# A 31-tap causal convolution rebuilt as three half-length filters on even and odd tokens, with a second u buffer and one weight remainder moved to VectorE

## The chip, the cores and the metric

The program runs on one core of one Trainium2 chip. The metric is the device time of one execution, in microseconds (us), median of several runs.

## The reference, cut to what matters

Three transformer-like blocks follow each other on a 1024 x 1024 activation (1024 tokens, width 1024, float32). The change lies in the input half of the second one: a wide projection, a gated product `a`, and a causal depthwise convolution of 31 taps over the tokens.

```python
    u = _rmsnorm(h, norm_g[l]) * (1.0 + scale) + shift
    proj = u @ w_in[l]
    ...
    a = conv_a * jax.nn.sigmoid(conv_bp)
    a = _causal_depthwise_conv(a, conv_w[l], conv_b[l])     # y[t] = b + sum_j w[j] * a[t - 30 + j], by channel
    a = jax.nn.silu(_layernorm(a, conv_ln_g[l], conv_ln_b[l]))
    a = a @ conv_pw[l]
    y_conv = a * jax.nn.silu(conv_gate)
    q = _rotary(q)
    k = _rotary(k) * (RET_QK_DIM ** -0.5)
    r = _retention_chunkwise(q, k, v)
```

## The kernel before

Activations lie with the channels on the 128 partitions and the tokens along the free dimension: eight tiles of 128 x 1024. A float32 product is made of three float32r matmuls of 128 x 512: weight high part by x high and by x low (L638, L639 in a mixed group), weight low part by x high (L640). ScalarE rounds a weight to its high part `whi` (L159); another engine subtracts to get the low part `wlo` (L160).

The wide projection of block 2 runs as 24 "mixed groups" (class `Mixed`). A group is two output tiles of 128 channels, computed by seven half-size products in place of eight, named a11, a12, s2, s1, s3, s4, a22 in the order in which they run. Each is 12 matmuls of 128 x 512. Products a11, s2, s3 and a22 accumulate in one bank `pb`; it is read out between them: ScalarE copies a11 into half of tile `g` (L653) and s2 into the other (L657), VectorE adds s3 to half of tile `u` (L650), and a22 goes to the other half of `u` (L1180). a12 and the pair s1, s4 use two banks `pa`: ScalarE copies s1 into `u` (L659), VectorE adds a12 and s4 to `g` (L650). So s4 can't begin before the copy of s1 into `u` is done.

The weights of a group come in two loads of 512 KB on SyncE's queue into `raw` (three buffers). GpSimd makes the sums that the products need, in place in `raw`: L607, L609 (s2), L612 (s4, over a12) and L615 (s3). From the third group on, GpSimd also makes all seven low parts (`on_pool = Mixed.ORDER`). `whi` and `wlo` hold two products each and have two buffers.

The groups come in this order: two gates, two "conv" groups, then six times a conv group and two of q, k, v, and two gates. After a conv group, VectorE multiplies the halves into `A[c]` (tile `cv`, L1201), a tile with 30 columns of zeros ahead of the tokens. After a q or k group, `turned` rotates g and u: eight products on VectorE (L1210 to L1214), four sums on GpSimd (L1213, L1215), and two stores on SyncE's queue, from g and u. Tile `g` has two buffers and `u` one.

The taps of the convolution fill VectorE's time between. Each tile c puts 31 jobs into the list `core.bg`, of which `worked` takes as many as `core.rate` says for each product: 2 for a product (RT = 8), 1.5 in q and k groups (RQ = 6). A job is one instruction of 128 x 1024 that multiplies a shifted `A[c]` by a column of weights and adds to an accumulator `acc` of two PSUM banks (L1149 for the first, L1153 for the others). A scheduler settles the order on each engine when the program is built; a job is only kept behind the latest matmul if on TensorE, and behind the latest paced gather if on VectorE.

Behind this stage come the retention loop, in which the convolved tiles are normalized over the channels (`ln_sum` to `ln_scale`), and a product with `conv_pw`.

Of the kernel before, what the change touches and what calls it, by code (L numbers as in the profile page):

```python
# [16 lines left out]
P = 128  # L17
S = 1024
# [11 lines left out]


SB = 6
RQ = 6
RT = 8
NS = 2
VA = 0
VB = 4
# [20 lines left out]
class Core:  # L58
# [40 lines left out]
        self.psm = self.lent.enter_context(self.tc.tile_pool(name=name, bufs=1, space=PSUM))  # L99

    def psum(self, tag, shape=(P, HALF)):
        pool, bufs = {"mm": (self.psm, 3), "acc": (self.psm, 1), "pa": (self.ps, 2), "pb": (self.ps, 2), "pc": (self.ps, 1)}[tag]
        return pool.tile(list(shape), F32, tag=tag, name=self.nm(tag), bufs=bufs)


# [1027 lines left out]
def block2(core, X, scratch, tabs, keep, after):  # L1133
# [7 lines left out]
    with ExitStack() as st:  # L1141
        cvp = st.enter_context(tc.tile_pool(name="b2_conv", bufs=1, reuse_waits="tile"))
        A = [cvp.tile([P, PAD + S], F32, tag=f"a{c}", name=f"cv_{c}") for c in range(KT)]

        def tap(c, j, state):
            def run():
                if j == 0:
                    state["acc"] = core.psum("acc", (P, S))
                    nc.vector.tensor_scalar(state["acc"], A[c][:, :S], core.vec("conv_w_2", c),  # L1149
                                            core.vec("conv_b_2", c), ALU.mult, ALU.add)  # L1150
                    return
                out = A[c][:, PAD:] if j == CW - 1 else state["acc"]
                nc.vector.scalar_tensor_tensor(out, A[c][:, j:j + S], core.vec("conv_w_2", j * KT + c), state["acc"],  # L1153
                                               ALU.mult, ALU.add)
            return run

        at = {}
        core.rate = RT
# [1 line left out]
        with tc.tile_pool(name="b2_mix", bufs=1, reuse_waits="tile") as pool:  # L1160
            cos = pool.tile([P, S], F32, tag="cos", name="cos")
            sin = pool.tile([P, S], F32, tag="sin", name="sin")
            nc.sync.dma_start(cos, ins["tab_cos"])
            nc.sync.dma_start(sin, ins["tab_sin"])
            temp = lambda: pool.tile([P, HALF], F32, tag="t", name=core.nm("rt"), bufs=2)
            turns = []

            def product(f, name):
                at[f, name] = mix.product(plan[f][2], name, x)

            def gather(f, name):
                kind, i, _ = plan[f]
                if name == "a11":
                    at[f, "g"] = tp.tile([P, S], F32, tag="g", name=core.nm("g"), bufs=2)
                if name == "s1":
                    at[f, "u"] = tp.tile([P, S], F32, tag="u", name=core.nm("u"), bufs=1)
                g, u = at[f, "g"], at.get((f, "u"))
                of = {"gate": AF.Silu, "conv": AF.Sigmoid}.get(kind, AF.Copy)
                mix.gather(name, at[f, name], (halves(g), halves(u) if u is not None else (None, None)),
                           lambda u1, ps: nc.scalar.activation(u1, ps, of))  # L1180
                if name in ("a12", "s3", "s4"):
                    core.paced = mix.last
                if kind == "gate":
                    if name == "s4":
                        gate(i, 0, g, slice(0, S))
                    elif name == "a22":
                        gate(i, 1, u, hs(1))
                elif name == "a22":
                    {"conv": conv, "q": turned, "k": turned, "v": values}[kind](kind, i, g, u)
                if name in ("a12", "s2"):  # L1190
                    while turns and len(turns) > (2 if name == "a12" else 0):
                        turns.pop(0)()

            def gate(i, k, y, rest):
                nc.scalar.activation(y[:, rest], y[:, rest], AF.Silu)
                nc.sync.dma_start(heads["gate"][i, :, k], y)

            def conv(_, c, a, b):
                nc.vector.memset(A[c][:, :PAD], 0.0)
                nc.scalar.activation(b[:, hs(1)], b[:, hs(1)], AF.Sigmoid)  # L1200
                nc.vector.tensor_tensor(A[c][:, PAD:], a, b, ALU.mult)  # L1201
                state = {}
                core.bg += [tap(c, j, state) for j in range(CW)]
                core.bg += [lambda: ready.append(c)]

            def turned(kind, i, a, b):
                for half in range(2):
                    sl = hs(half)
                    t1, t2 = temp(), temp()
                    nc.vector.tensor_tensor(t1, a[:, sl], sin[:, sl], ALU.mult)  # L1210
                    nc.vector.tensor_tensor(a[:, sl], a[:, sl], cos[:, sl], ALU.mult)
                    nc.vector.tensor_tensor(t2, b[:, sl], sin[:, sl], ALU.mult)
                    nc.gpsimd.tensor_tensor(a[:, sl], a[:, sl], t2, ALU.subtract)  # L1213
                    nc.vector.tensor_tensor(b[:, sl], b[:, sl], cos[:, sl], ALU.mult)  # L1214
                    nc.gpsimd.tensor_tensor(b[:, sl], b[:, sl], t1, ALU.add)  # L1215
# [12 lines left out]

            ready = []
            mix.early(product, gather)  # L1230
            mix.on_pool = Mixed.ORDER
            for f in range(2, len(plan) - 1):
                core.rate = RQ if plan[f][0] in "qk" else RT
                for name in Mixed.ORDER:
                    product(f, name)
                    gather(f, name)

            f += 1
            core.rate = RT
# [12 lines left out]
            for name in ("s4", "a22"):  # L1252
                gather(f, name)
            while turns:
                turns.pop(0)()
            core.paced = None
            core.drain()
        scratch["mixed"].close()
        core.banks()
        with tc.tile_pool(name="b2_ret", bufs=1, reuse_waits="tile") as pool:  # L1260
            ln = {}

            def ln_sum(c):
                if c == 0:
                    return
                if c == 1:
                    ln["acc"] = pool.tile([P, S], F32, tag="lnacc", name="ln_acc")
                nc.gpsimd.tensor_tensor(ln["acc"], A[0][:, PAD:] if c == 1 else ln["acc"], A[c][:, PAD:], ALU.add)

            def ln_mean():  # L1270
                ln["mu"] = pool.tile([P, S], F32, tag="lnmu", name="ln_mu")
# [3 lines left out]
                    nc.scalar.activation(ln["mu"][:, hs(half)], mu, AF.Copy)  # L1275

            def ln_center(c):
                a = A[c][:, PAD:]
                nc.vector.tensor_tensor(a, a, ln["mu"], ALU.subtract)
                if c == 0:  # L1280
                    ln["var"] = pool.tile([P, S], F32, tag="lnacc", name="ln_var")
                    nc.scalar.activation(ln["var"], a, AF.Square)
                else:
                    sq = core.raw()
                    nc.scalar.activation(sq, a, AF.Square)
                    nc.gpsimd.tensor_tensor(ln["var"], ln["var"], sq, ALU.add)

            def ln_rstd():
# [6 lines left out]
                ln["rb"] = core.over_partitions(ln["r"], pool, tag="lnmu")  # L1295

            def ln_scale(c):
                a = A[c][:, PAD:]
                nc.vector.tensor_tensor(a, a, ln["rb"], ALU.mult)
                nc.scalar.activation(a, a, AF.Silu, bias=core.vec("conv_ln_b_2", c), scale=core.vec("conv_ln_g_2", c))  # L1300

            om = pool.tile([P, P], F32, tag="onesm", name="onesm")
# [137 lines left out]
            core.rate = 0  # L1440
        for half in range(2):
            for c in range(KT):
                core.split(X[c][:, 0, hs(half)], X[c][:, 1, hs(half)], A[c][:, PAD + half * HALF:PAD + (half + 1) * HALF])
        st.close()
        gp = keep.enter_context(tc.tile_pool(name="b2_g", bufs=1, side="right", reuse_waits="tile"))
        G = [gp.tile([P, 2, S], R32, tag=f"g{c}", name=f"yc_{c}") for c in range(KT)]
# [1217 lines left out]
```

## Time and profile before

| | |
|---|---|
| runs of the kernel | 3717.8, 3723.08, 3727.68 us; median 3723.08 |
| profiled execution | 3721.68 us, span of the trace 3719.8 us, mean granted clock 0.961 |
| busy, share of the span | TensorE 93%, its weight loads 75%, VectorE 70%, GpSimd 46%, ScalarE 42% |
| the stage of the 22 looped groups | from 1612 to 2110 us of the span |

The span runs from the first to the last instruction of the trace; 1.9 us of the execution lie around it. TensorE is busy through nearly all of it, so what a stage costs beyond its matmuls is read from TensorE's waits and from its granted clock in that stage.

### The profile page before, as it was taken

To read this page: it belongs to the slowest core of one execution; us is meant where nothing else is said; L and a number is where in the kernel's file an instruction comes from. 1 tells how busy PE (TensorE), PEld (TensorE's weight loads), DVE (VectorE), ACT (ScalarE), POOL (GpSimd) and SP (SyncE) were. 2 spreads that over 40 slices of the span, in tenths; PEclk is the share of its full clock that TensorE was granted. 3 is DMA by queue.
4 is the path that set the end of the run, shared out by engine and by line. 5 is a ranking of instruction groups with operands and counts; after the bars stand their busy time and mean duration, and the time that the engine had idled before them with its cause. 6 is when DMAs were issued, how large, how long until landed. Compare 5 with 4: busy or idle time off the path is not lost.

```text
span 3719.8 us, 45673 instructions
## 1 busy us (share of the span) xinstructions
PE 3448.3 (93%) x16540; PEld 2777.5 (75%) x16540; DVE 2604.3 (70%) x3332; ACT 1567.2 (42%) x2737; POOL 1714.2 (46%) x1398
## 2 busy tenths in 40 slices
PE   8999989899998999899889989889898999899998
PEld 7878777777776778677667778668676788677776
DVE  7888897777776655759988765774559765655644
ACT  5666674433334444532223344224443235553335
POOL 2343343456554533567777653434556442431122
PEclk9999999999999999899999999999899999899999
DMA  4101016333325423322222354466352344325513
GB/s 144 38 30 38 28 63 223 119 107 103 96 94 184 125 74 119 108 80 74 77 76 69 122 156 130 116 194 201 128 161 86 92 122 128 102 80 181 181 48 111
DMA packets 431132, 409.84 MB, mean 110 GB/s; under 512 B 34059, under 2 KB 364347, under 8 KB 430907
## 3 DMA queue, kind: packets, MB, share of 16 engines
q1 hardware_dynamic: 396164, 330.27, 28.8%
q0 software_dynamic: 21088, 68.19, 5.1%
q10 hardware_dynamic: 13655, 8.46, 0.8%
q8 instruction: 131, 2.15, 0.2%
q14 instruction: 94, 0.77, 0.1%
HBM read 284.80 MB, written 122.03 MB: 109 GB/s over the span
## 4 chain that ended last, share of the span: by engine, by line
PE 63%; DVE 15%; DMA 8%; POOL 6%; issue 5%; ACT 3%; SPq 0%; ACTq 0%; POOLq 0%; DVEq 0%
PE mm L236 10%; PE mm L234 10%; PE mm L235 10%; PE pb L638 4%; PE pb L640 4%; PE pb L639 4%; DVE wlo L160 3%; PE pa L638 3%; PE pa L640 3%; PE pa L639 3%; POOL wlo L160 2%; DMA raw<-in_w_in_dram 1%; DMA zy<-zraw_dram 1%; ACT whi L159 1%; DVE x L160 1%
## 5 line engine op out<-in xcount | busy, mean ns | idle before, releaser
L159 ACT ACTIVATE whi<-raw 128x512 fp32r<-128x512 f32 (+3 forms) x610 | 431.8, 737 | 802.1 <-PE pb L639 188.5
L160 DVE TENSOR_TENSOR wlo<-raw,whi 128x512 fp32r<-128x512 f32 (+3 forms) x402 | 503.8, 1273 | 187.9 <-ACT whi L159 184.9
L234 PE MATMUL mm<-x,whi 128*128 128x512 f32 x1152 | 462.7, 402 | 9.0 <-ACT whi L159 3.6
L236 PE MATMUL mm<-x,wlo 128*128 128x512 f32 x1152 | 458.4, 399 | 6.0 <-DVE wlo L160 6.0
L235 PE MATMUL mm<-x,whi 128*128 128x512 f32 x1152 | 460.9, 400 | 0.5 <-DVE x L163 0.2
L160 POOL TENSOR_TENSOR wlo<-raw,whi 128x512 fp32r<-128x512 f32 x208 | 288.0, 1403 | 116.5 <-ACT whi L159 116.4
L493 POOL TENSOR_TENSOR s<-s,f 128x127 f32<-128x127 f32 (+1 forms) x192 | 194.3, 1019 | 293.7 <-DVE f L492 187.4
L1153 DVE SCALAR_TENSOR_TENSOR acc<-cv,par,acc 128x1024 f32<-128x1024 f32 x232 | 298.0, 1285 | 4.3
L638 PE MATMUL pa<-x,whi 128*128 128x512 f32 x648 | 261.1, 403 | 19.5 <-ACT u L659 12.3
L234 PE MATMUL mm<-yc,whi 128*128 128x512 f32 (+1 forms) x656 | 267.8, 409 | 7.3 <-ACT whi L159 6.0
L235 PE MATMUL mm<-yc,whi 128*128 128x512 f32 (+1 forms) x656 | 265.5, 405 | 5.6 <-DVE yc L160 5.5
L640 PE MATMUL pa<-x,wlo 128*128 128x512 f32 x648 | 260.0, 401 | 9.9 <-DVE wlo L160 9.8
L236 PE MATMUL mm<-yc,wlo 128*128 128x512 f32 (+1 forms) x656 | 264.6, 405 | 3.6 <-DVE wlo L160 3.5
L639 PE MATMUL pa<-x,whi 128*128 128x512 f32 x648 | 259.2, 400 | 6.6 <-DVE x L160 6.6
L640 PE MATMUL pb<-x,wlo 128*128 128x512 f32 x576 | 234.2, 412 | 29.8 <-POOL wlo L160 21.6
L234 PEld LDWEIGHTS mm<-x,whi 128*128 128x128 f32 x1152 | 220.0, 191 | 55.6 <-ACT whi L159 4.1
L638 PE MATMUL pb<-x,whi 128*128 128x512 f32 x576 | 237.2, 412 | 25.8 <-ACT whi L159 8.8
L236 PEld LDWEIGHTS mm<-x,wlo 128*128 128x128 f32 x1152 | 219.2, 190 | 52.9 <-DVE wlo L160 7.5
L235 PEld LDWEIGHTS mm<-x,whi 128*128 128x128 f32 x1152 | 219.8, 191 | 45.5 <-DVE x L163 0.6
L639 PE MATMUL pb<-x,whi 128*128 128x512 f32 x576 | 235.1, 408 | 3.5 <-DVE x L160 3.5
L492 DVE TENSOR_TENSOR_SCAN f<-f 128x128 f32<-128x128 f32 (+1 forms) x192 | 195.7, 1033 | 39.0 <-ACT f L485 37.9
L607 POOL TENSOR_TENSOR raw<-raw 128x512 f32<-128x512 f32 x66 | 92.5, 1402 | 275.3 <-DMA raw<-in_ffn_w_in_dram 131.6
(617 smaller groups left out, 8355.2 us busy)
## 6 DMA issues: line engine op xcount, KB each, us to landing
raw<-in_w_in_dram SPq DMA_DIRECT2D x96, 512.0 KB
raw<-in_ffn_w_in_dram SPq DMA_DIRECT2D x44, 512.0 KB
raw<-in_w_out_dram SPq DMA_DIRECT2D x32, 512.0 KB
g<-g_dram SPq DMA_DIRECT2D x56, 256.0 KB
raw<-in_sb_w_in_dram SPq DMA_DIRECT2D x24, 512.0 KB
raw<-in_ada_w_dram SPq DMA_DIRECT2D x24, 512.0 KB
raw<-h_dram SPq DMA_DIRECT2D x18, 512.0 KB
g_dram<-t POOLq DMA_DIRECT2D x8, 1024.0 KB, 4.7
```

Source lines behind the costliest of these rows:

```text
L159: nc.scalar.activation(hi, src, AF.Copy)
L160: return (eng or nc.vector).tensor_tensor(lo, src, hi.bitcast(F32), ALU.subtract).ins
L234: nc.tensor.matmul(ps, w_h, x[:, 0, sl], start=start and k == 0, stop=False)
L235: nc.tensor.matmul(ps, w_h, x[:, 1, sl], start=False, stop=False)
L236: self.last = nc.tensor.matmul(ps, w_l, x[:, 0, sl], start=False, stop=stop and k == n - 1).ins
L492: nc.vector.tensor_tensor_scan(rev, rev, rev, 1.0, ALU.mult, ALU.bypass)
L493: nc.gpsimd.tensor_tensor(s[:, :m - 1], s[:, :m - 1], f[:, 1:m], ALU.mult)
L607: self.eng.tensor_tensor(at["s1"], at["a21"], at["a22"], ALU.add)
L638: nc.tensor.matmul(ps, hi[:, i], x[i][:, 0], start=first and i == 0, stop=False, skip_group_check=more)
L639: nc.tensor.matmul(ps, hi[:, i], x[i][:, 1], start=False, stop=False, skip_group_check=more)
L640: self.core.last = nc.tensor.matmul(ps, lo[:, i], x[i][:, 0], start=False, stop=i == self.N - 1, skip_group_check=more).ins
L1153: nc.vector.scalar_tensor_tensor(out, A[c][:, j:j + S], core.vec("conv_w_2", j * KT + c), state["acc"], ALU.mult, ALU.add)
```

## The change

The 31 taps on 1024 tokens become three filters on 512. `A[c]` holds the even tokens and the odd tokens apart, each with 15 zeros ahead. With x0, x1 the two sequences and o = -(w1, w3, ...) on x1 plus the bias, the program computes the even outputs from the even taps (16) on x0 minus o (15 taps), and the odd outputs from the sums of neighbouring taps (16) on x0 + x1, corrected by the same two filters. It takes 15 + 16 + 16 taps of 128 x 512, and of these the first of the odd and the first of the even filter go to ScalarE (`odd_first`, `even_first`); `sums`, `both` and `even` are four further VectorE instructions, one of them on a single column. Four small VectorE instructions prepare the weights once. Each accumulator is now one PSUM bank (`acc0`, `acc1`). The rates rise to RT = 12 and RQ = 9, since a tile now gives 49 jobs. The steps behind (`ln_*`, `core.split`) read `A[c]` in the new order, and the last one puts the tokens back in order as it writes.

Besides, tile `u` of the mixed groups gets a second buffer, and the low part of product a12 is made by VectorE, not GpSimd.

```diff
-RQ = 6
-RT = 8
+RQ = 9
+RT = 12
...
-        def tap(c, j, state):
-            def run():
-                if j == 0:
-                    state["acc"] = core.psum("acc", (P, S))
-                    nc.vector.tensor_scalar(state["acc"], A[c][:, :S], core.vec("conv_w_2", c),
-                                            core.vec("conv_b_2", c), ALU.mult, ALU.add)
-                    return
-                out = A[c][:, PAD:] if j == CW - 1 else state["acc"]
-                nc.vector.scalar_tensor_tensor(out, A[c][:, j:j + S], core.vec("conv_w_2", j * KT + c), state["acc"],
-                                               ALU.mult, ALU.add)
-            return run
+        def taps(c):
+
+            x0, x1, y0, y1 = (t[:, e] for t in (apart(A[c]), inner[c]) for e in range(2))
...
+            def odd_first():
+                st["o"] = core.psum("acc0")
+                nc.scalar.activation(st["o"], x1[:, 1:1 + HALF], AF.Identity, scale=wn[:, 0, c:c + 1], bias=bias)
+
+            def even_first():
+                st["e"] = core.psum("acc1")
+                nc.scalar.activation(st["e"], x0[:, :HALF], AF.Identity, scale=wd[:, 0, c:c + 1])
+
+            def tap(key, x, at, w, out=None):
+                o = st[key]
+                nc.vector.scalar_tensor_tensor(o if out is None else out, x[:, at:at + HALF], w, o, ALU.mult, ALU.add)
+
+            def sums():
+                nc.vector.tensor_tensor(x1, x0, x1, ALU.add)
+
+            def both():
+                nc.vector.tensor_tensor(st["e"], st["o"], y0, ALU.subtract)
+
+            def even():
+                nc.vector.tensor_scalar(y0[:, :1], y0[:, :1], bias, None, ALU.add)
+                nc.vector.scalar_tensor_tensor(y0[:, 1:], y0[:, 1:], b2[:, c:c + 1], st["o"][:, :HALF - 1], ALU.add, ALU.subtract)
...
+            at = len(jobs) - 4
+            jobs[at] = lambda f=jobs[at]: (f(), even_first())
...
-                    at[f, "u"] = tp.tile([P, S], F32, tag="u", name=core.nm("u"), bufs=1)
+                    at[f, "u"] = tp.tile([P, S], F32, tag="u", name=core.nm("u"), bufs=2)
...
-                nc.vector.tensor_tensor(A[c][:, PAD:], a, b, ALU.mult)
...
+                by_turn = lambda t: t.rearrange("p (n e) -> p e n", e=2)
+                nc.vector.tensor_tensor(inner[c], by_turn(a), by_turn(b), ALU.mult)
+                core.bg += taps(c)
...
-            mix.on_pool = Mixed.ORDER
+            mix.on_pool = tuple(n for n in Mixed.ORDER if n != "a12")
...
-                core.split(X[c][:, 0, hs(half)], X[c][:, 1, hs(half)], A[c][:, PAD + half * HALF:PAD + (half + 1) * HALF])
+                n = slice(half * HALF // 2, (half + 1) * HALF // 2)
+                core.split(*(X[c][:, i, hs(half)].rearrange("p (n e) -> p e n", e=2) for i in range(2)), inner[c][:, :, n])
```

On GpSimd, around the end of the first k group and the start of the next one (`raw_14227` and `raw_14191` are the weights of that next group, `g_14057` and `g_14087` the k tile that is rotated), the order before was:

```order
L1215 TENSOR_TENSOR u_13963<-u_13963,rt_14026 128x512
L607 TENSOR_TENSOR raw_14232<-raw_14232 128x4x128
L609 TENSOR_TENSOR raw_14191<-raw_14232,raw_14191 128x4x128
L160 TENSOR_TENSOR wlo_14213<-raw_14191,whi_14212 128x512 x2
L612 TENSOR_TENSOR raw_14191<-raw_14191 128x4x128
L160 TENSOR_TENSOR wlo_14254<-raw_14232,whi_14253 128x512
L615 TENSOR_TENSOR raw_14191<-raw_14232,raw_14191 128x4x128
L1213 TENSOR_TENSOR g_14057<-g_14057,rt_14174 128x512
```

and with the change it is:

```order
L1256 TENSOR_TENSOR u_13990<-u_13990,rt_14055 128x512
L607 TENSOR_TENSOR raw_14270<-raw_14270 128x4x128
L609 TENSOR_TENSOR raw_14227<-raw_14270,raw_14227 128x4x128
L612 TENSOR_TENSOR raw_14227<-raw_14227 128x4x128
L160 TENSOR_TENSOR wlo_14250<-raw_14227,whi_14249 128x512
L615 TENSOR_TENSOR raw_14227<-raw_14270,raw_14227 128x4x128
L160 TENSOR_TENSOR wlo_14293<-raw_14270,whi_14292 128x512
L1254 TENSOR_TENSOR g_14087<-g_14087,rt_14210 128x512
```

One of the two low parts of the pair is gone from the row with `x2`, and L612, which writes over a12's weights, now stands right behind L609.

On VectorE, in the same k group, the order before was:

```order
L650 TENSOR_TENSOR u_14115<-u_14115,pb_14042 128x512
L1153 SCALAR_TENSOR_TENSOR acc_13960<-cv_13213,par,acc_13960 128x1024
L650 TENSOR_TENSOR g_14057<-g_14057,pa_14101 128x512
L1153 SCALAR_TENSOR_TENSOR acc_13960<-cv_13213,par,acc_13960 128x1024 x3
L1212 TENSOR_TENSOR rt_14174<-u_14115,sin 128x512
L1153 SCALAR_TENSOR_TENSOR acc_13960<-cv_13213,par,acc_13960 128x1024
L1214 TENSOR_TENSOR u_14115<-u_14115,cos 128x512
L650 TENSOR_TENSOR g_14210<-g_14210,pa_14216 128x512
```

and with the change:

```order
L650 TENSOR_TENSOR u_14149<-u_14149,pb_14071 128x512
L1175 SCALAR_TENSOR_TENSOR acc_2451_14106<-cv_13213,par,acc_2451_14106 128x512
L1175 SCALAR_TENSOR_TENSOR acc_2437_13988<-cv_13213,cv_wn,acc_2437_13988 128x512
L1175 SCALAR_TENSOR_TENSOR acc_2451_14106<-cv_13213,par,acc_2451_14106 128x512
L650 TENSOR_TENSOR g_14087<-g_14087,pa_14134 128x512
L1178 TENSOR_TENSOR cv_13213<-cv_13213 128x527
L160 TENSOR_TENSOR wlo_14250<-raw_14227,whi_14249 128x512
L1175 SCALAR_TENSOR_TENSOR acc_2451_14106<-cv_13213,par,acc_2451_14106 128x512 x4
L1253 TENSOR_TENSOR rt_14210<-u_14149,sin 128x512
L1175 SCALAR_TENSOR_TENSOR acc_2451_14106<-cv_13213,par,acc_2451_14106 128x512
L1255 TENSOR_TENSOR u_14149<-u_14149,cos 128x512
L650 TENSOR_TENSOR g_14247<-g_14247,pa_14253 128x512
```

The taps are half as long, and a12's low part of the next group (`wlo_14250`) stands among them, behind the gather of s4.

On ScalarE, in a later group, the first tap of tile 5 now stands between the copy of s1 and the next high parts:

```order
L657 ACTIVATE g_15535<-pb_15519 128x512
L659 ACTIVATE u_15598<-pa_15582 128x512
L1167 ACTIVATE acc_2638_15755<-cv_13217,par,cv_wn 128x512
L159 ACTIVATE whi_15676<-raw_15674 128x512 x2
L159 ACTIVATE whi_15721<-raw_15674 128x512
L159 ACTIVATE whi_15721<-raw_15717 128x512
L1221 ACTIVATE u_15598<-pb_15519 128x512
```

There are sixteen such rows of L1167 and L1171 in the stage, and none before; each writes an accumulator that VectorE must have let go.

## Rows read from the trace of the kernel before

**Rows 1.** Windows: busy us of each engine (instructions), PEclk, DMA share, GB/s.

```profile
1612.00:1685.00 73.00, 73.00 (x320) 59.62 (x319) 52.77 (x48) 26.69 (x45) 55.82 (x42) 1.00 0.21 62
...
1612.00:2110.00 498.00, 455.15 (x1885) 359.00 (x1884) 437.49 (x390) 154.43 (x268) 376.30 (x272) 0.95 0.24 74
```

**Rows 2.** Waits of TensorE in 1612 to 2110: total us, times, longest.

```profile
PE pb L640 <- POOL wlo L160: 25.9, 15, 4.3
PE pa L638 <- ACT u L659: 10.1, 5, 3.6
PE pb L638 <- ACT whi L159: 6.2, 7, 2.1
```

**Rows 3.** A group of TensorE instructions there: count | busy, mean ns | idle before.

```profile
L640 PE MATMUL pb<-x,wlo 128*128 128x512 f32 x85 | 39.8, 469 | 21.6 <-POOL wlo L160 21.6
```

**Rows 4.** Timeline of TensorE after a wait: start us, us, instruction, idle before.

```profile
1704.29 0.59 PE L640 MATMUL pb<-x,wlo 128*128 128x512 f32 x1 [2.40 <-POOL wlo L160]
1704.68 0.63 PE L638 MATMUL pb<-x,whi 128*128 128x512 f32 x1
1705.11 0.63 PE L639 MATMUL pb<-x,whi 128*128 128x512 f32 x1
```

**Rows 5.** Timeline of GpSimd just before that wait ends.

```profile
1699.48 1.29 POOL L1213 TENSOR_TENSOR g<-g,rt 128x512 f32<-128x512 f32 x1 [0.63 <-DVE g L1211]
1700.73 3.50 POOL L160 TENSOR_TENSOR wlo<-raw,whi 128x512 fp32r<-128x512 f32 x2
```

**Rows 6.** A group of GpSimd instructions in 1612 to 2110.

```profile
L160 POOL TENSOR_TENSOR wlo<-raw,whi 128x512 fp32r<-128x512 f32 x151 | 212.7, 1427 | 75.4 <-ACT whi L159 75.2
```

**Rows 7.** Waits of ScalarE in 1612 to 2110.

```profile
ACT whi L159 <- PE pb L639: 84.6, 29, 6.4
...
ACT g L653 <- DMA q_dram<-g: 17.3, 2, 11.0
...
ACT g L653 <- DMA k_dram<-g: 10.9, 1, 10.9
...
ACT u L659 <- DMA q_dram<-u: 8.4, 3, 6.1
...
ACT u L659 <- DMA k_dram<-u: 6.5, 3, 4.2
```

**Rows 8.** Groups of VectorE instructions in 1612 to 2110.

```profile
L1153 DVE SCALAR_TENSOR_TENSOR acc<-cv,par,acc 128x1024 f32<-128x1024 f32 x232 | 298.0, 1285 | 4.3
L650 DVE TENSOR_TENSOR g<-g,pa 128x512 f32<-128x512 f32 x44 | 30.0, 682 | 36.3 <-PE pa L640 33.2 <-issue 2.8
...
L1149 DVE TENSOR_SCALAR acc<-cv,par 128x1024 f32<-128x1024 f32 x8 | 10.8, 1344 | 0.2
L1153 DVE SCALAR_TENSOR_TENSOR cv<-cv,par,acc 128x1024 f32<-128x1024 f32 x8 | 10.2, 1278 | 0.2
```

**Rows 9.** Lines on single sources: duration ns min/median/max, first and last start.

```profile
L1153 DVE SCALAR_TENSOR_TENSOR acc<-cv,par,acc x232: 1272/1289/1291, 1636.4 to 2106.5; 128x1024 f32<-128x1024 f32 x116
...
L1210 DVE TENSOR_TENSOR rt<-g,sin x16: 677/1283/1779, 1676.0 to 2056.1; 128x512 f32<-128x512 f32 x16
...
L1201 DVE TENSOR_TENSOR cv<-g,u x8: 1215/1979/2324, 1632.6 to 2033.2; 128x1024 f32<-128x1024 f32 x8
```

**Rows 10.** Groups elsewhere in the kernel that stand for new instructions.

```profile
L2108 DVE SCALAR_TENSOR_TENSOR xbc<-xc,par,xbc 128x512 f32<-128x512 f32 x24 | 17.4, 747 | 0.4
...
L160 DVE TENSOR_TENSOR wlo<-raw,whi 128x512 fp32r<-128x512 f32 x2 | 1.3, 688 | 3.4 <-ACT whi L159 3.4
...
L612 POOL TENSOR_TENSOR raw<-raw 128x512 f32<-128x512 f32 x66 | 101.0, 1530 | 30.0 <-DVE wlo L160 27.9
...
L2402 ACT ACTIVATE mm<-mm,par 128x512 f32<-128x512 f32 x16 | 10.6, 660 | 17.4 <-PE mm L236 17.3
...
L159 ACT ACTIVATE yc<-raw 128x1024 fp32r<-128x1024 f32 x8 | 15.9, 2008 | 5.2 <-DMA raw<-ys_dram 5.2
...
L159 ACT ACTIVATE x<-raw 128x1024 fp32r<-128x1024 f32 x15 | 15.9, 1060 | 27.9 <-DMA raw<-yret_dram 26.6 <-DMA raw<-o_dram 1.1
```

More of the change, by code (lines that the diff above doesn't have):

```diff
@@ L101, in psum @@
     def psum(self, tag, shape=(P, HALF)):
-        pool, bufs = {"mm": (self.psm, 3), "acc": (self.psm, 1), "pa": (self.ps, 2), "pb": (self.ps, 2), "pc": (self.ps, 1)}[tag]
+        pool, bufs = {"mm": (self.psm, 3), "acc0": (self.psm, 1), "acc1": (self.psm, 1), "pa": (self.ps, 2), "pb": (self.ps, 2), "pc": (self.ps, 1)}[tag]
         return pool.tile(list(shape), F32, tag=tag, name=self.nm(tag), bufs=bufs)
@@ L1143, in block2 @@
         A = [cvp.tile([P, PAD + S], F32, tag=f"a{c}", name=f"cv_{c}") for c in range(KT)]
-        def tap(c, j, state):
-            def run():
-                if j == 0:
-                    state["acc"] = core.psum("acc", (P, S))
-                    nc.vector.tensor_scalar(state["acc"], A[c][:, :S], core.vec("conv_w_2", c),
-                                            core.vec("conv_b_2", c), ALU.mult, ALU.add)
-                    return
-                out = A[c][:, PAD:] if j == CW - 1 else state["acc"]
-                nc.vector.scalar_tensor_tensor(out, A[c][:, j:j + S], core.vec("conv_w_2", j * KT + c), state["acc"],
-                                               ALU.mult, ALU.add)
-            return run
+        apart = lambda t: t.rearrange("p (e n) -> p e n", e=2)
@@ new lines, in block2 @@
+        inner = [apart(a)[:, :, PAD // 2:] for a in A]
+        wd = core.vec("conv_w_2", 0, CW * KT).rearrange("p (j c) -> p j c", c=KT)
+        wn = cvp.tile([P, CW // 2, KT], F32, tag="wn", name="cv_wn")
+        ws = cvp.tile([P, CW // 2 + 1, KT], F32, tag="ws", name="cv_ws")
+        b2 = cvp.tile([P, KT], F32, tag="b2", name="cv_b2")
+        nc.vector.tensor_scalar(wn, wd[:, 1::2], -1.0, None, ALU.mult)
+        nc.vector.tensor_copy(ws[:, 0], wd[:, 0])
+        nc.vector.tensor_tensor(ws[:, 1:], wd[:, 2::2], wd[:, 1::2], ALU.add)
@@ new lines, in block2 @@
+        nc.vector.tensor_scalar(b2, core.vec("conv_b_2", 0, KT), 2.0, None, ALU.mult)
+        def taps(c):
+            x0, x1, y0, y1 = (t[:, e] for t in (apart(A[c]), inner[c]) for e in range(2))
+            bias = core.vec("conv_b_2", c)
+            st = {}
+            def odd_first():
[14 more added lines that the diff above has]
+                nc.vector.scalar_tensor_tensor(y0[:, 1:], y0[:, 1:], b2[:, c:c + 1], st["o"][:, :HALF - 1], ALU.add, ALU.subtract)
+            n = CW // 2
+            jobs = [odd_first]
+            jobs += [lambda m=m: tap("o", x1, 1 + m, wn[:, m, c:c + 1]) for m in range(1, n)]
+            at = len(jobs) - 4
+            jobs[at] = lambda f=jobs[at]: (f(), even_first())
+            jobs += [sums]
+            jobs += [lambda m=m: tap("e", x0, m, wd[:, 2 * m, c:c + 1], y0 if m == n else None) for m in range(1, n + 1)]
+            jobs += [both, even]
+            jobs += [lambda m=m: tap("e", x1, m, ws[:, m, c:c + 1], y1 if m == n else None) for m in range(n + 1)]
+            return jobs
@@ L1198, in conv @@
             def conv(_, c, a, b):
-                nc.vector.memset(A[c][:, :PAD], 0.0)
+                nc.vector.memset(apart(A[c])[:, :, :PAD // 2], 0.0)
                 nc.scalar.activation(b[:, hs(1)], b[:, hs(1)], AF.Sigmoid)
-                nc.vector.tensor_tensor(A[c][:, PAD:], a, b, ALU.mult)
-                state = {}
-                core.bg += [tap(c, j, state) for j in range(CW)]
+                by_turn = lambda t: t.rearrange("p (n e) -> p e n", e=2)
+                nc.vector.tensor_tensor(inner[c], by_turn(a), by_turn(b), ALU.mult)
+                core.bg += taps(c)
                 core.bg += [lambda: ready.append(c)]
@@ L1267, in ln_sum @@
                     ln["acc"] = pool.tile([P, S], F32, tag="lnacc", name="ln_acc")
-                nc.gpsimd.tensor_tensor(ln["acc"], A[0][:, PAD:] if c == 1 else ln["acc"], A[c][:, PAD:], ALU.add)
+                acc = apart(ln["acc"])
+                nc.gpsimd.tensor_tensor(acc, inner[0] if c == 1 else acc, inner[c], ALU.add)
             def ln_mean():
@@ L1277, in ln_center @@
             def ln_center(c):
-                a = A[c][:, PAD:]
-                nc.vector.tensor_tensor(a, a, ln["mu"], ALU.subtract)
+                a = inner[c]
+                nc.vector.tensor_tensor(a, a, apart(ln["mu"]), ALU.subtract)
                 if c == 0:
                     ln["var"] = pool.tile([P, S], F32, tag="lnacc", name="ln_var")
-                    nc.scalar.activation(ln["var"], a, AF.Square)
+                    nc.scalar.activation(apart(ln["var"]), a, AF.Square)
                 else:
                     sq = core.raw()
-                    nc.scalar.activation(sq, a, AF.Square)
+                    nc.scalar.activation(apart(sq), a, AF.Square)
                     nc.gpsimd.tensor_tensor(ln["var"], ln["var"], sq, ALU.add)
@@ L1297, in ln_scale @@
             def ln_scale(c):
-                a = A[c][:, PAD:]
-                nc.vector.tensor_tensor(a, a, ln["rb"], ALU.mult)
+                a = inner[c]
+                nc.vector.tensor_tensor(a, a, apart(ln["rb"]), ALU.mult)
                 nc.scalar.activation(a, a, AF.Silu, bias=core.vec("conv_ln_b_2", c), scale=core.vec("conv_ln_g_2", c))
```

## Prediction, written before the changed kernel ran

> **What bounds the kernel now.** Three questions, in this order: is TensorE the bound of the stage that changes, what does it wait for there, and is the engine that is relieved the one it waits for?
>
> First the windows of the stage [rows 1]. Until 1685 us TensorE is busy without a gap at a granted clock of 1.00 (the level of 2.4 GHz): 320 instructions in 73.00 us, 0.228 us each. Over the whole stage it is busy 455.15 of 498 us, at 0.95. The 22 groups hold 22 x 84 = 1848 products; at 0.228 us these are 421 us, and some 8 us of transposes bring it to 430. So 68 us of the 498 are not products at full speed. 43 us of them are gaps (498 - 455.15), the other 25 go to the clock: 0.05 of 498. A stall and the clock belong together: after a wait of 2.40 us the next products start 0.43 us apart instead of 0.228, so at the level of 1.2 GHz [rows 4]. Per microsecond of gap the clock costs 25/43 = 0.58 us more.
>
> Second, the waits of TensorE [rows 2]: 25.9 us for a low part from GpSimd, 10.1 us at s4 for ScalarE's copy of s1 into `u`, 6.2 us for a high part. None is for VectorE. Of the 25.9 us, 21.6 fall on the first product of a group, a11, whose x is a tile `x` in bank `pb` [rows 3]. GpSimd's timeline ahead of one shows why: a rotation's sum and two low parts in a row, without idle time between, a11's among the last [rows 5].
>
> Third, the engine loads. GpSimd is busy 376 us, of which 151 recorded low parts make 212.7, at 1.427 us each [rows 1, 6]. VectorE is busy 437 us, 88%, more than GpSimd; but it is not late: ahead of 44 gathers it idles 36.3 us, 33.2 of them for TensorE [rows 8]. ScalarE has the time (154 us busy) and loses it in order: it waits 84.6 us for TensorE to let go of a high part's buffer, and 14.9 us (8.4 + 6.5) ahead of the copy into `u` until the store of the old `u` has landed [rows 7].
>
> **The convolution.** Before, VectorE spends 298.0 + 10.8 + 10.2 = 319.0 us on 248 taps [rows 8]. A tap of half the length isn't in this trace under that line; the same instruction on 128 x 512 takes 0.747 us elsewhere [rows 10], more than half of 1.285. A tile now takes 45 taps and one instruction like them in `even`: 46 x 0.747 = 34.4 us. `both` is a sum with one PSUM operand, 0.68 as a gather [rows 8], the single column about 0.1. `sums` reads two SBUF operands, as the rotation does: 0.677 to 1.779 us, median 1.283 [rows 9]; I take the median. That is 36.5 us a tile, 292 for eight, 27 us less than before.
>
> The gated product now reads its operands with a step of two elements. Before it took 1.215 to 2.324 us, by the median 8 x 1.979 = 16 us [rows 9]. A ScalarE pass with a far larger step takes 2008 ns against 1060 [rows 10], so the bound is +16 us on VectorE; below nothing it can't go, as the elements are the same. I take no change, since a step of two is nearer to none, and keep 16 for the range. The last `core.split` has the same bound on sixteen instructions of ScalarE and VectorE each; they lie beside the retention loop. The Trainium skill, "SBUF — State Buffer", section on the DMA port swizzle, says that two hits in a line of 16 bytes are enough for full rate, which two float32 of four are; by it the term is nothing. No run here shows it yet.
>
> **The low part that moves.** GpSimd loses 22 x 1.427 = 31 us. VectorE gains 22 instructions with two SBUF operands: 0.688 us when GpSimd is quiet [rows 10], 1.283 by the rotation's median [rows 9], so 15 to 28 us; I take 28, since GpSimd is busy for three quarters of the stage [rows 1]. VectorE's account then closes at +1 us (-27 + 28), between -12 and +17 with the range of the gated product: the shorter convolution pays for the low part and brings nothing by itself.
>
> That a row with two SBUF operands spreads from 677 to 1779 ns, while a tap with its accumulator in PSUM keeps to 1272 to 1291 [rows 9], is contention. The Trainium skill, "GPSIMD Engine Reference", section "Key points", states the rule: GpSimd contends with VectorE instructions that have two SBUF inputs. The trace agrees. The rule speaks against this part of the change, as the moved low part is such an instruction and the removed taps were not.
>
> GpSimd gets some of its 31 us back as waits: L612 overwrites a12's weights, so it must now wait for VectorE's low part. In the feed-forward stage, whose 44 groups make their low parts on VectorE, L612 idles 27.9 us for that [rows 10], 0.63 a group; for 22 groups 14 us. So about half of the relief stays.
>
> What this is worth to TensorE: it has 15 waits of 25.9 us, at most one low part (1.427) can go from each, 21.4 us; half of that is **10.7 us**. Bounds: 0 and 21.4.
>
> **The second `u`.** The copy of s1 no longer waits for the store of the group before, and the 10.1 us at s4 go: **10.1 us**. What is late next is the same wait on `g`, two buffers already, 28.2 us in three waits of ScalarE [rows 7]; it stays, and TensorE has no wait that ends with it [rows 2]. Lower bound 0, if `g` takes it over.
>
> **The clock.** 20.8 us fewer gaps at 0.58: **12.1 us**; bounds 0 and 0.58 times the bounds above.
>
> **What it adds to the path.** Sixteen first taps on ScalarE stand between high parts. 660 ns is the nearest row [rows 10], 16 x 0.66 = 10.6 us. TensorE does wait for high parts already, and behind such a tap the next `whi` waits, so I charge them in full: **+10.6 us**; hidden, they cost 0. The four preparing instructions (some 1 us) lie ahead of the stage. The jobs end with the last group: the 21 groups behind the first conv group take 13 x 21 + 8 x 15.75 = 399 of the 8 x 50 = 400, so the retention stage gets no backlog.
>
> **Sum.** -10.7 - 10.1 - 12.1 + 10.6 = -22.3 us. The profiled execution took 3721.68 us, 1.4 under the median of 3723.08; 3721.7 - 22.3 = 3699.4, rounded to **3700**.
>
> **The rivals.**
>
> *Nothing to measure.* `g`'s store takes the place of `u`'s, and VectorE's low parts are as late as GpSimd's were. For it: the 28.2 us on `g`, and L612's wait in the feed-forward stage. Against it: TensorE's waits end with `u`, never with `g`. It leaves perhaps 5 us of gaps and 3 of clock, given back by the first taps: -8 to +3 us, 3714 to 3725.
>
> *Slower: ScalarE waits for VectorE.* A first tap needs an accumulator that VectorE releases some taps into the tile before. VectorE is 88% busy; if it is k taps late where ScalarE meets the tap, ScalarE stands 0.747 k us, and every high part behind it. Sixteen places: the 22 us are used up at 1.4 us a place, about two taps late, and at three taps (2.2 us, 36 us) the time is 3721.7 - 22 + 36 = 3736. For it: VectorE's load and the in-order ScalarE. Against it: VectorE now is early at its gathers, 36.3 us of idle time.
>
> *Much faster.* The low parts come in time, the first taps lie in ScalarE's idle time: 21.4 + 10.1 gaps and 18.3 of clock, 50 us, 3672. For it: ScalarE idles two thirds of the stage. Against it: both waits would have to vanish whole in groups where VectorE and GpSimd also rotate.
>
> *By the contention rule*, a mechanism of its own: each moved low part stretches a GpSimd instruction from 1.29 to about 1.75 us (two low parts together 3.50 against the sum's 1.29 alone, [rows 5]). 22 x 0.46 = 10 us more of GpSimd; with L612's 14 only 7 of 31 us stay, a quarter and not half: the first term is 5 us, the clock 9, and the time 3708. This is the Trainium skill's rule of the section above; it stays on the faster side and is part of the forecast's case.
>
> **How the numbers follow.** About 0.3%, 11 us, is what a measurement of this kernel can tell from no change. The forecast's case (-12 to -40 us, the contention rule in it): 0.60. Much faster, beyond -40: 0.16. Nothing to measure: 0.15. Slower: 0.09. So faster 0.76, same 0.15, slower 0.09. The range leaves out the upper part of "slower" and the lower half of "much faster": 3674 to 3725.
>
> **What would show it.** Right: no wait of ScalarE's L659 on a store; TensorE's waits for `wlo` down from 25.9 to about 15 us; the stage near 476 us at a clock of 0.97; taps near 0.747 us; `wlo` of VectorE near 1.28 us there, and L612 waiting for it. Wrong: waits of ScalarE's L1167 or L1171 on VectorE of more than a microsecond each, followed by TensorE's waits for `whi`; a gated product of 3 us; gathers of VectorE that TensorE waits for; or the gap on `u` come back on `g`.

## The result, and the profile after

The changed kernel takes 3676.18 us (median of 4 runs, 3674.56 to 3680.41), the kernel before 3725.38 us (4 runs): a ratio of 0.9875, with a 95% interval from 0.9859 to 0.9891. That is 49 us less, where 22 were forecast; it lies nearest to the rival "much faster" (3672). The profiled executions' spans are 3719.8 and 3674.8 us.

The stage first, as in [rows 1]: TensorE's last mixed product begins at 2070.6 us, and the first product of the retention stage at 2081. (In the kernel before, the last mixed product begins at 2119.2 us, a little behind the window of [rows 1], with 26 instructions of later products ahead of it.)

```profile
1612.00:2081.00 469.00, 440.56 (x1902) 353.25 (x1900) 432.26 (x566) 168.41 (x290) 362.32 (x258) 0.98 0.27 83
```

The granted clock rose from 0.95 to 0.98, and VectorE's busy time hardly moved (437.49 to 432.26 us). TensorE's waits in that window answer to [rows 2]:

```profile
PE pb L638 <- DVE u L650: 10.8, 6, 4.1
PE pb L640 <- POOL wlo L160: 3.6, 5, 1.8
PE pc L1264 <- DVE g L650: 2.2, 1, 2.2
PE pa L640 <- POOL wlo L160: 1.8, 3, 0.7
```

The wait for the copy into `u` is gone, as forecast. The wait for GpSimd's low parts fell from 25.9 to 5.4 us, where 15 was forecast. In their place stands one for VectorE's gathers (10.8 us), which the prediction had listed as a sign of being wrong. One more wait lies at the end of the stage. TensorE's timeline there:

```profile
2070.60 0.63 PE L640 MATMUL pb<-t,wlo 128*128 128x512 f32 x1
2081.32 0.76 PE L234 MATMUL mm<-x,whi 128*128 128x512 f32 x1 [10.09 <-DVE cv L1175]
2081.88 0.63 PE L235 MATMUL mm<-x,whi 128*128 128x512 f32 x1
```

and VectorE's, with the last tap of the convolution:

```profile
2078.91 1.48 DVE L1175 SCALAR_TENSOR_TENSOR acc<-cv,cv_ws,acc 128x512 f32<-128x512 f32 x2
2080.42 0.75 DVE L1175 SCALAR_TENSOR_TENSOR cv<-cv,cv_ws,acc 128x512 f32<-128x512 f32 x1
```

The first product of the next stage wants the accumulator's bank, and the taps are not through. The prediction excluded this backlog.

GpSimd's groups in 1612 to 2110 answer to [rows 6]:

```profile
L160 POOL TENSOR_TENSOR wlo<-raw,whi 128x512 fp32r<-128x512 f32 x131 | 183.9, 1420 | 35.1 <-ACT whi L159 35.1
...
L612 POOL TENSOR_TENSOR raw<-raw 128x512 f32<-128x512 f32 x21 | 27.2, 1296 | 8.5 <-DVE wlo L160 7.9
```

ScalarE's waits in the stage answer to [rows 7]. No line of it waits for a store any more, on `u` or on `g`; the first taps L1167 and L1171 wait for VectorE instead, 13.2 + 11.6 us in eight waits (a ninth, for the gated product, is 1.5 us):

```profile
ACT u L659 <- PE pa L640: 16.3, 14, 1.7
ACT acc L1167 <- DVE cv L1185: 13.2, 4, 3.9
...
ACT acc L1171 <- DVE cv L1175: 11.6, 4, 5.7
```

The prices of the new instructions, from the lines on single sources (ns min/median/max):

```profile
L1175 DVE SCALAR_TENSOR_TENSOR acc<-cv,cv_wn,acc x112: 740/748/757, 1635.9 to 2040.0; 128x512 f32<-128x512 f32 x112
...
L1167 ACT ACTIVATE acc<-cv,par,cv_wn x8: 767/782/783, 1635.1 to 2003.2; 128x512 f32<-128x512 f32 x8
...
L1171 ACT ACTIVATE acc<-cv,par x8: 672/692/695, 1635.8 to 2029.2; 128x512 f32<-128x512 f32 x8
...
L1243 DVE TENSOR_TENSOR cv<-g,u x8: 1244/1508/1892, 1633.7 to 1985.0; 128x1024 f32<-128x1024 f32 x8
...
L160 DVE TENSOR_TENSOR wlo<-raw,whi x23: 679/1184/2533, 1627.3 to 2073.0; 128x512 fp32r<-128x512 f32 x21, 128x1024 fp32r<-128x1024 f32 x2
```

The last row mixes two shapes. The 21 instructions of 128 x 512 are a12's low parts: 679 to 1775 ns, 1080 at the median. The two of 128 x 1024 run at the end of the stage, and the 2533 ns are one of theirs.

### The profile page after: what moved, and what is told of

Read it like the earlier page. It is cut to its first block, busy times and chain, and to the rows that moved or that the text cites. A ratio compares the mean times of both kernels' runs of the same rounds, so it can differ in the third digit from the quotient of the medians.

```text
span 3674.8 us, 45863 instructions
## 1 busy us (share of the span) xinstructions
PE 3423.6 (93%) x16540; PEld 2769.0 (75%) x16540; DVE 2599.2 (71%) x3502; ACT 1577.6 (43%) x2753; POOL 1679.4 (46%) x1376
## 4 chain that ended last, share of the span: by engine, by line
PE 34%; DVE 10%; DMA 3%; POOL 3%; issue 2%; ACT 2%; ACTq 0%; POOLq 0%; DVEq 0%; SPq 0%
PE mm L236 6%; PE mm L235 6%; PE mm L234 6%; DVE acc L1175 2%; PE pb L640 1%; PE pb L638 1%; POOL wlo L160 1%; PE pb L639 1%; PE pa L638 1%; PE pa L639 1%; PE pa L640 1%; DVE wlo L160 1%; DVE s_H L1936 1%; PE pc L1430 1%; PE pa L1434 1%
## 5 line engine op out<-in xcount | busy, mean ns | idle before, releaser
L160 DVE TENSOR_TENSOR wlo<-raw,whi 128x512 fp32r<-128x512 f32 (+3 forms) x424 | 533.1, 1276 | 186.6 <-ACT whi L159 183.8
L234 PE MATMUL mm<-x,whi 128*128 128x512 f32 x1152 | 462.0, 402 | 19.3 <-DVE cv L1175 10.1
L160 POOL TENSOR_TENSOR wlo<-raw,whi 128x512 fp32r<-128x512 f32 x186 | 257.1, 1400 | 76.7 <-ACT whi L159 76.7
L234 PEld LDWEIGHTS mm<-x,whi 128*128 128x128 f32 x1152 | 220.0, 191 | 66.7 <-issue 10.8
L638 PE MATMUL pb<-x,whi 128*128 128x512 f32 x576 | 232.8, 405 | 20.1 <-ACT g L657 6.4
L639 PE MATMUL pb<-x,whi 128*128 128x512 f32 x576 | 231.0, 401 | 3.0 <-DVE x L160 3.0
L640 PEld LDWEIGHTS pa<-x,wlo 128*128 128x128 f32 x648 | 123.4, 190 | 46.9 <-DVE wlo L160 17.3
```

The source lines that it names most:

```text
L160: return (eng or nc.vector).tensor_tensor(lo, src, hi.bitcast(F32), ALU.subtract).ins
L234: nc.tensor.matmul(ps, w_h, x[:, 0, sl], start=start and k == 0, stop=False)
L638: nc.tensor.matmul(ps, hi[:, i], x[i][:, 0], start=first and i == 0, stop=False, skip_group_check=more)
L639: nc.tensor.matmul(ps, hi[:, i], x[i][:, 1], start=False, stop=False, skip_group_check=more)
L640: self.core.last = nc.tensor.matmul(ps, lo[:, i], x[i][:, 0], start=False, stop=i == self.N - 1, skip_group_check=more).ins
```

## The experiments

After the result it was open which of the three parts brings the 49 us. One theory: each part brings what the prediction gave it, only larger. Its rival, to which the first results led: the second `u` brings nearly all, since TensorE's waits that are named after GpSimd's low parts are a consequence of the single `u`.

### One part alone, on the kernel before

`u_only` gives `u` its second buffer and nothing else; `a12_only` makes a12's low part on VectorE and nothing else; `u_a12` is both; `conv_only` is the changed kernel with those two lines as before.

```
u_only, u_a12:    tag="u", ... bufs=1   ->  bufs=2
a12_only, u_a12:  mix.on_pool = Mixed.ORDER  ->  tuple(n for n in Mixed.ORDER if n != "a12")
conv_only:        the convolution and RT, RQ of the change; bufs=1; on_pool = Mixed.ORDER
```

> The second u buffer alone. Theory 1: the waits of TensorE at s4 for ScalarE's copy into u (10.1 us) go with their share of the clock, about -16 us, 3709; the copy no longer waits for a store. Theory 2: the wait moves to g or to GpSimd's low part, 0 to -5 us.

> a12's low part on VectorE alone, with the long taps. Theory 1: the waits for GpSimd's low parts halve at least, -17 us with the clock and up to -34, so 3690 to 3708. Theory 2: VectorE has 15 to 28 us more to do in a stage in which it was 88% busy, and without the shorter convolution this shows: no gain or up to 15 us slower, with TensorE waiting for VectorE's gathers.

> The second u and a12's low part on VectorE, with the old convolution. Theory 1: most of the 49 us, 3680 to 3695. Theory 2: VectorE bounds the stage, at most -15 us, 3710 or above.

> The convolution alone on the kernel before: three half-length filters, rates 12 and 9; u keeps one buffer and GpSimd keeps a12's low part. Theory 1 (the gain is GpSimd's relief and the second u, the convolution only pays VectorE's bill): TensorE's waits for GpSimd's low parts and for the copy into u stay near 26 and 10 us, the time stays within 10 us of before, about 3720. Theory 2 (the gain is the convolution: 27 us less of VectorE and shorter instructions in its queue): 3685 to 3700, and both waits shrink though nothing was done to them.

Measured beside one kernel before (3724.16 us): `u_only` 3683.64 us, ratio 0.9892 [0.9873, 0.9910]; `a12_only` 3727.29 us, 1.0006 [0.9994, 1.0019]; `u_a12` 3683.51 us, 0.9887 [0.9866, 0.9907]; `conv_only` 3730.25 us, 1.0021 [1.0010, 1.0033].

So the second `u` by itself saves 40.5 us, the low part by itself nothing, and the convolution by itself costs 6 us. No theory on record for `u_only` gave it more than 16 us. In the trace of `conv_only` TensorE stands 11.1 us for the last tap at the end of the stage, which it doesn't in the kernel before, so its cost can lie in the rate of the jobs and not in the filters. The waits of TensorE in `u_only` and 1612 to 2110 us show that the low parts come in time though GpSimd still makes every one of them:

```profile
PE pa L1367 <- DMA k<-k_dram: 11.7, 1, 11.7
PE pb L638 <- DVE u L650: 6.4, 4, 4.1
PE pb L640 <- POOL wlo L160: 6.4, 3, 3.1
PE pa L640 <- POOL wlo L160: 3.5, 4, 1.5
```

They cost 9.9 us instead of 25.9. The 11.7 us stand behind the stage: the last mixed product begins at 2069.1 us, no later than in the changed kernel (2070.6), and then TensorE waits for a load of k, where the changed kernel waits 10.1 us for the last tap. So within the stage the second `u` alone gains what the whole change gains. In the trace of `u_a12` the last mixed product begins at 2061.3 us, 8 us earlier; this is lost again in the retention stage, where TensorE waits 12.9 us for that load and 4.6 for VectorE (11.7 and 0.6 in `u_only`). In `a12_only` GpSimd has 22 low parts less, and TensorE's wait for its low parts hardly moves:

```profile
PE pb L640 <- POOL wlo L160: 23.2, 15, 4.6
PE pa L638 <- ACT u L659: 12.8, 4, 4.7
...
PE pa L640 <- DVE wlo L160: 3.9, 2, 3.2
```

The moved low parts add 3.9 us of their own, so the waits for low parts of either engine are 27.1 us.

GpSimd's own group there shows where the relief went: into waiting for ScalarE's high parts, 98.1 us where it was 75.2 [rows 6].

```profile
L160 POOL TENSOR_TENSOR wlo<-raw,whi 128x512 fp32r<-128x512 f32 x129 | 187.3, 1469 | 98.1 <-ACT whi L159 98.1
```

### The change less one part

```
conv_u:    after with on_pool = Mixed.ORDER  (GpSimd makes a12's low part again)
conv_a12:  after with bufs=1 for "u"
first_dve: after, and in odd_first and even_first
-  nc.scalar.activation(st["o"], x1[:, 1:1 + HALF], AF.Identity, scale=wn[:, 0, c:c + 1], bias=bias)
+  nc.vector.tensor_scalar(st["o"], x1[:, 1:1 + HALF], wn[:, 0, c:c + 1], bias, ALU.mult, ALU.add)
rates_14_10: after with RQ = 10, RT = 14 in place of 9, 12
```

> The changed kernel with a12's low part back on GpSimd: the new convolution and the second u. So far the second u alone gave 40 us, the low part and the convolution alone nothing. Theory 1 (the low part earns nothing in any company, since GpSimd was not the bound): 3672 to 3682, as the changed kernel. Theory 2 (with the second u GpSimd is the next bound, and its relief is what the rest of the change gives): 3686 or more, with TensorE's waits for GpSimd's low parts back at 10 us or more.

> The changed kernel with one u buffer: the new convolution and the low part on VectorE. If the second u is the whole mechanism: 3720 to 3735, TensorE's waits for the copy into u and for low parts near 40 us as before. If the three parts need each other and the first two carry a share: 3700 to 3715.

> The changed kernel with the two first taps of each tile on VectorE as tensor_scalar, so that ScalarE never waits for an accumulator. The prediction charged 10.6 us for them on ScalarE. If they cost that: 3664 to 3670. If they are hidden, or if their waits (25 us of ScalarE in the profile) land on idle time: VectorE takes 16 x 0.7 = 11 us more, and as the last tap ends the stage, the time is the same to 10 us slower, 3676 to 3686.

> The changed kernel with RT = 14 and RQ = 10, so that the jobs are handed out faster and the last tile's taps come earlier. In the changed kernel the first product of the retention stage waits 10.1 us for the last tap, whose bank it takes. If this wait is what the hand-out of jobs causes, it goes: -8 to -16 us with the clock, 3660 to 3668. If VectorE is full to the end whatever the rate: 3672 to 3680, and the wait stays.

Measured beside one kernel before (3720.5 us): `conv_u` 3687.31 us, 0.9908 [0.9893, 0.9923]; `conv_a12` 3738.94 us, 1.0048 [1.0035, 1.0060]; `first_dve` 3681.09 us, 0.9891 [0.9877, 0.9904]; `rates_14_10` 3670.86 us, 0.9860 [0.9847, 0.9874].

With one `u` the other two parts together make the kernel slower; all of the gain stands on the second `u`. (3738.94 us lies above both ranges put on record for `conv_a12`.) First taps on VectorE bring nothing, and in the changed kernel no wait of TensorE ends with a high part: nothing in these traces shows that ScalarE's first taps cost TensorE time. Against `conv_u` the moved low part is worth some 12 us (0.9908 - 0.9875 = 0.0033), but not where it was priced. The time of `conv_u` is that of its second theory, the waits are those of the first: TensorE's waits for low parts are 6.3 us in `conv_u` and 5.4 in the changed kernel, and both begin the stage behind retention within 1 us of each other (2304.6 and 2303.6). Of the 10.1 us between their spans, 7.1 are a wait in that later stage, here in `conv_u` in 2300 to 2420:

```profile
PE mm L235 <- DVE yc L160: 7.7, 1, 7.7
```

In the changed kernel the same products wait 0.6 us for such a low part. The instructions of TensorE stand in another order ahead of it (the two kernels have the same order from 2389 us of the changed kernel's trace to the end), though the change touches no line of that stage. What part of this the moved low part causes wasn't tried.

### The end of the stage, and the copy of s1

```
after_same:  the changed kernel once more
rates_again: rates_14_10 once more
rates_16_12: after with RQ = 12, RT = 16
s1_dve: before, with
+        self.copy = lambda out, ps: core.nc.scalar.activation(out, ps, AF.Copy)
...
-            nc.scalar.activation(u2, ps, AF.Copy)
+            self.copy(u2, ps)
...
+            mix.copy = nc.vector.tensor_copy
```

> The changed kernel once more, beside its variants on one chip: 3672 to 3681.

> The rates 14 and 10 once more beside the changed kernel: 4 to 10 us below it if the wait for the last tap was worth its 10 us, equal if the earlier difference was that of two chips.

> Rates 16 and 12: the jobs come earlier still. If an early last tap is all that counts, the time equals that of 14 and 10, 3665 to 3672. If taps handed out faster stand ahead of the gathers that TensorE needs, TensorE's waits for VectorE's gathers grow and the time is above the changed kernel's.

> The kernel before with one u buffer, but in the looped groups VectorE, not ScalarE, copies s1 into u. Theory 1 (the wait for the store of u stands in ScalarE's in-order queue ahead of the next high parts, and TensorE's waits for GpSimd's low parts are its echo): ScalarE no longer waits for a store of u, GpSimd's waits for high parts fall from 75 us to 40 or less, TensorE's waits for low parts from 25.9 to 15 or less, though GpSimd makes as many low parts as before; VectorE now waits for the store, and the time is 3695 to 3720. Theory 2 (GpSimd's own load sets these waits): they stay at 20 us or more.

Measured beside one kernel before (3722.84 us): `after_same` 3679.6 us, 0.9875 [0.9858, 0.9892]; `rates_again` 3675.82 us, 0.9864 [0.9849, 0.9879]; `rates_16_12` 3669.89 us, 0.9849 [0.9835, 0.9863]; `s1_dve` 3740.0 us, 1.0038 [1.0023, 1.0053].

More jobs per product end the convolution inside the stage. With 16 and 12 the last tap begins at 2042.8 us:

```profile
L1175 DVE SCALAR_TENSOR_TENSOR cv<-cv,cv_ws,acc x8: 735/736/750, 1693.2 to 2042.8; 128x512 f32<-128x512 f32 x8
```

No product waits for it there; the stage behind retention begins at 2285.7 us, 18 us earlier than in the changed kernel's trace. At the end 10 us of it are left (3679.6 - 3669.89; the intervals of the two ratios overlap by 0.0005). With 14 and 10 it is 3.8 us (3679.6 - 3675.82), which the intervals don't tell from none; some is lost where `conv_u` lost its time, in `rates_again` in 2300 to 2420:

```profile
PE mm L235 <- DVE yc L160: 5.9, 2, 3.8
```

`rates_16_12` has the lowest ratio of all that ran; it isn't clear of that with 14 and 10.

`s1_dve` was to test how the wait for `u` reaches the low parts: by the theory of that moment through ScalarE, whose high parts stand behind its stalled copy. With the copy on VectorE, TensorE's waits for low parts should have shrunk. They did not:

```profile
PE pb L641 <- POOL wlo L160: 26.4, 16, 5.0
PE pa L639 <- DVE u L660: 15.1, 4, 6.1
```

That theory fell (ScalarE still waited 12.9 us for stores of `g` there, so its queue isn't cleared of every part). What does go with the waits is the order of TensorE's products. Where `u` has one buffer, the scheduler places the next group's a11 ahead of this group's s4 in most groups. This is one such place, TensorE's order in `u_only` (+) against before (-); `pb_14195` is a11 of the next group, `pa_14101` s4:

```
+L638 MATMUL pa_14101<-x_6581,whi_14119 128x512
...
+L640 MATMUL pa_14101<-x_6587,wlo_14120 128x512
 L638 MATMUL pb_14195<-x_6580,whi_14154 128x512
...
 L640 MATMUL pb_14195<-x_6586,wlo_14155 128x512
-L638 MATMUL pa_14101<-x_6581,whi_14119 128x512
...
-L640 MATMUL pa_14101<-x_6587,wlo_14120 128x512
```

Counted over the 22 groups of the stage (in the groups that aren't in the fourth column only the first two of a11's twelve instructions stand ahead), with TensorE's waits for GpSimd's low parts in 1612 to 2110:

| kernel | buffers of `u` | groups with a11 ahead of s4 | of these, all of a11 ahead | waits for GpSimd's low parts, us |
|---|---|---|---|---|
| before | 1 | 16 | 12 | 25.9 |
| conv_only | 1 | 16 | 12 | 32.0 |
| a12_only | 1 | 15 | 12 | 23.2 (and 3.9 for VectorE's) |
| conv_a12 | 1 | 15 | 12 | 18.8 (and 12.9 for VectorE's) |
| s1_dve | 1 | 15 | 11 | 26.4 |
| u_only | 2 | 6 | 0 | 9.9 |
| u_a12 | 2 | 8 | 0 | 4.9 |
| conv_u | 2 | 5 | 0 | 6.3 |
| after | 2 | 6 | 0 | 5.4 |
| rates_16_12 | 2 | 7 | 0 | 7.0 |

It holds within the kernel before, too. The 21.6 us that a11 waits for low parts [rows 3] are eleven waits, and all eleven stand at places where the whole of a11 is ahead of s4; at the other ten places a11 waits for none. The three waits of ScalarE for stores of `g` [rows 7] are copies of an a11 that stands ahead in this way.

The timeline of all engines before, at the longest but one of the fifteen waits, shows how a wait for the store can become one for a low part:

```profile
1914.75 1.15 ACT L159 ACTIVATE whi<-raw 128x512 fp32r<-128x512 f32 x2 [3.88 <-POOL wlo L160]
1914.89 1.29 POOL L1213 TENSOR_TENSOR g<-g,rt 128x512 f32<-128x512 f32 x1 [0.63 <-DVE g L1211]
...
1917.82 1.26 POOL L1215 TENSOR_TENSOR u<-u,rt 128x512 f32<-128x512 f32 x1
...
1919.04 2.95 POOL L160 TENSOR_TENSOR wlo<-raw,whi 128x512 fp32r<-128x512 f32 x2
1919.10 0.34 SPq L1217 DMA_DIRECT2D q_dram<-u  x1
...
1920.80 0.79 PE L640 MATMUL pb<-x,wlo 128*128 128x512 f32 x1 [4.11 <-POOL wlo L160]
...
1921.97 0.60 ACT L659 ACTIVATE u<-pa 128x512 f32<-128x512 f32 x1 [6.07 <-DMA q_dram<-u]
```

The old `u` is rotated on GpSimd until 1919.08, its store is issued at 1919.10, and ScalarE copies s1 into `u` at 1921.97; s4 can't begin before. TensorE, sent to a11 instead, meets it before GpSimd, which does the rotation first, has made its low part. Had the order not been changed, TensorE would have stood at s4 for the store, so here the gap is the store's either way and only its label is GpSimd's. Of the eleven places this can be read so at two, here and at 2065.5 us, where the copy of s1 waits 4.2 us for the store of a k tile. At five, ScalarE copies the moved a11 into `g` before it comes to s1, so the copy comes late by that order; at the other four it waits for no store. So at most places it is the order, settled when the program is built for one `u`, that goes with the wait, and not a store that is late in the trace. This is read from order and trace; a kernel with one `u` and the other order was not run.

## Why the prediction was right and wrong

**The number: right by luck.** 3676 us lies 2 us above the lower end of the range, 24 us from the 3700 of the sum. What saved it is that the range took in half of the rival "much faster". Its signs came true, low parts in time and first taps hidden, but not by the relief of GpSimd that it was priced with.

**What bounds the stage: failed in one reading.** "25.9 us for a low part from GpSimd" was taken for GpSimd's load. The sign against it stood in the rows themselves: GpSimd idled 75.2 us for ScalarE [rows 6], and an engine that sets the pace would not idle so long. What the runs showed in its place: 22 low parts less leave the waits where they were (`a12_only`), a second `u` takes them from 25.9 to 9.9 us. The Trainium skill, "Perfetto Trace Analysis", section "Optimization Strategy", says that a gap that repeats on the engine that should be saturated can mean too few buffers for the next tile. The runs agree: fifteen waits, 1.7 us on average, and with the second `u` seven (9.9 us).

**The low part: the step that failed.** The sum gave it 10.7 us and 10.7 x 0.58 = 6.2 of clock; alone it brings 0 (`a12_only`), beside the second `u` 0 in the time (`u_a12` against `u_only`), the 8 us within the stage being lost behind it. What it costs the engines was not underrated: 1.080 us at the median for 1.283 taken, and L612's waits for it 7.9 us for 14. The moved low parts spread from 679 to 1775 ns. The Trainium skill, "GPSIMD Engine Reference", section "Key points", says that GpSimd contends with VectorE instructions that have two SBUF inputs. The spread agrees.

**The second `u`: right as far as it went, mis-sized.** 10.1 us and 5.9 of clock were summed; `u_only` measured 40.5. Of the 25.9 us of the term above, 16 went with the second `u` alone. That one buffer also settles the order of TensorE's products was not thought of. "It stays" was said of ScalarE's 28.2 us for stores of `g`, and they went too, though `g` has two buffers as before. The rival that `g` takes the place of `u` is thus out.

**The clock: right in kind.** Gaps down, clock up, 0.95 to 0.98, where 0.97 was forecast. By the prediction's own reckoning the gaps of the stage fell from 43 to 28 us (469 - 440.56) and the clock's share from 25 to some 9 (0.02 of 469), an estimate: about one for one, where 0.58 was taken.

**The convolution: right as it was run.** It brings nothing by itself, +6 us alone, of which the wait for the last tap can be the cause. With rates 16 and 12 the kernel is below `u_a12`, which has the old taps (0.9849 [0.9835, 0.9863] against 0.9887 [0.9866, 0.9907]), so it may be worth something when its jobs come early; the old taps at a higher rate were not run. The tap was forecast at 0.747 us and is 0.748 at the median. The gated product with a step of two takes 1508 ns at the median for 1979 before [rows 9], and 1244 for 1215 at the least, so nothing of the 16 us kept for the range. By the Trainium skill, "SBUF — State Buffer", section on the DMA port swizzle, the term is nothing. The trace agrees.

**The first taps: charged 10.6 us, none of it seen.** They take 782 and 692 ns, more than the 660 taken, but ScalarE had the time. The rival "ScalarE waits for VectorE" came true in its first half (eight waits, 3.1 us each on average) and not in its second: TensorE has no wait for a high part in the stage. The other sign of being wrong, TensorE waiting for VectorE's gathers, came true too, with 10.8 us.

**"No backlog": failed.** 399 of 400 jobs counts when jobs are issued, not when VectorE has done them. The wait of 10.1 us is the price; higher rates remove it, and with 16 and 12 the time is 10 us lower.

**The sum.** Of the 49 us, 40.5 are the second `u`'s. Some 9 are left for the other two parts in its company, which the intervals of `u_only` (0.9873 to 0.9910) and of the changed kernel (0.9859 to 0.9891) don't tell from none. By spans, 31.4 of 45.0 us are gained by the start of the stage behind retention (2335.0 to 2303.6) and the rest in stages that the change doesn't touch. Why these gain is open.

## What to carry to other kernels

The label of a wait names the last link only: before an engine is relieved, see whether it idles itself, and whether the scheduler moved the waiting product there because another one was blocked. A tile with one buffer that the next accumulation needs, be it held by a store or by the order that the scheduler makes around it, is the first candidate for a second one; try it alone, before work is moved between engines. A background queue whose accumulators lie in banks that the next stage takes must be done, not only issued, when the stage ends.

## What the runs showed of the hardware

A sum of two SBUF operands on VectorE takes 0.68 us beside a quiet GpSimd [rows 10] and up to three times that beside a busy one; near the end of the stage VectorE's timeline has one at 2.00 us:

```profile
2076.14 2.00 DVE L160 TENSOR_TENSOR x<-rt,x 128x512 fp32r<-128x512 f32 x1
```

GpSimd runs sums of 128x1024 there, four in 10.79 us. In the changed kernel's stage, the rotations' products and the low parts (L160), all of 128x512, take 675 to 686 ns in the thirteen cases in which no GpSimd instruction overlaps them, and up to 2.00 us otherwise. The taps between, with their accumulator in PSUM, keep to 740 to 757 ns. On ScalarE a first tap with a scale from SBUF takes 692 ns and one with scale and bias 782, 90 ns more.
